# Decoder trunk on one core: memory heads and heads at other places of the second value stage, S1's output weights summed in SBUF, residual rows scaled on GpSimd

## The chip, the cores and the metric

The kernel runs on one core of a Trainium2 chip. The metric is the device time of one execution in microseconds (us), lower is better. The engines are called as the profile calls them: PE (TensorE, matrix products; PEld its weight loads), DVE (VectorE), ACT (ScalarE), POOL (GpSimd) and SP (SyncE, which here only issues DMAs). POOL also issues DMAs; only those can add to what lies at their target (accumulate).

## The reference

Two layers of a decoder over one sequence of 512 positions with 2048 columns, all in fp32:

```python
def hybrid_layer(h, mem, w_in, b_forget, w_mem_kv, w_out, ln_gain, ln_bias):
    p = h @ w_in                       # 2048 columns to all heads' parts and three small ones
    y_fox = forgetting_attention(q, k, v, cumsum(log_sigmoid(f_logit + b_forget)))   # 6 heads of 128
    y_dsa = sparse_attention(rope(q), rope(k), v, top_k of the index scores)         # 6 heads
    y_mem = attention(q, *split(mem @ w_mem_kv))                                     # 4 heads, 256 memory tokens
    y = concatenate([y_fox, y_dsa, y_mem]) * silu(gates)                             # 512 x 2048
    return layer_norm(ALPHA * h + y @ w_out, ln_gain, ln_bias)
```

A query of the sparse heads sees the 128 keys with the highest index score at most. Layer 2 takes layer 1's output.

## The kernel before

**Products.** PE multiplies a number as a high and a low part (`hi`, `lo`), so one fp32 product is three matmuls; ACT makes the high part of a weight (`whi<-raw`), DVE the low part (`wlo<-raw,whi`). In the trace these matmuls are triples such as z<-whi,yh, z<-wlo,yh, z<-whi,yl. The two large stages, the values (with gates and the projections that lie among them, PSUM tiles `v`) and the output projection (`z`), multiply 2 x 2 blocks with seven products instead of eight, whose names are P1, P7, Q6, Q4, P2, Q5, Q3. Some of them take a sum of weight blocks: `T1`, the right operand of Q5 (whose left operand is S1), is the sum of two blocks, as is `T3`, the operand of P7. Q6 and Q4 take a sum that grows from P7's (`grown`: an accumulating DMA of POOL adds a block to a tile in SBUF).

**Weights.** They stream in chunks of two halves; a half is 128 x 1024 (512 KB). `load_w` issues a chunk's load on SP (tiles `raw`) two chunks ahead of use, and the split runs three halves ahead. For the value stage's pairs 1 to 5, `pair_w` loads both blocks of a sum and DVE adds them (`raw<-raw,other`). For the value stage's pair 0 and all of the output stage, the sums are made in DRAM (`weight_sums`): POOL copies a block of 1 MB to a DRAM tile `sum` and later adds the other to it with an accumulating DMA; the halves are then loaded from `sum`. `paced` spreads these steps over the stages, and outside the first value stage each has a `pool_waits` ahead of it: DVE writes `mark`, POOL reads it into `seen`, so that POOL's queue goes no further than DVE has come.

**Stages of a layer.** Small and index products; the first value stage (`VAL_FIRST`, in all pairs P1, P7, P2, Q6, Q4); the second (`VAL_SECOND`, Q5 and Q3 of pairs 0 to 5, two chunks each, 24 in all, 24 matmuls each); the q and k projections of the heads that are not in the value products, with the attention heads run among them (the heads stage, tiles `c`, `s`, `pt`, `po`); the output stage (`OUT_ORDER`, steps of two chunks); the layer norm. In layer 2's first value stage `residual_rows` loads 12 tiles of layer 1's result, multiplies each by a row of gains and adds a row of biases (`scale_row`, on DVE) and writes it back with a POOL DMA.

**Heads.** A memory head (`mem_head`) loads its q by a turning DMA (DMA_TRANSPOSE on SP), splits it, multiplies by the memory keys (`sm`), turns the softmax's values on PE (`ptm`) and multiplies by the memory values (`po`). The others do the same with `s`, `pt` and `po`; `load_qk` and `load_ck` fetch their inputs on SP. `start_heads` queues the heads in the order of the table `START`. Memory heads 0 to 2 are queued at Q3 of pairs 1, 3 and 5, memory head 3 is the seventh in `START`.

**Order.** The program of each engine is written out once, at build time. `Clock` keeps an estimate of each engine's time; `flow` queues a generator of steps, and `advance`, called after each triple of matmuls or so, emits steps of queued work when their engine is due. So a head queued sooner moves its matmuls between other matmuls. On each engine, and on the two DMA queues, instructions go in program order. In the output stage `load_res` loads x's tiles (`z<-in_x_dram`, in layer 2 `z<-x`) on POOL, DVE adds them to the product (`z<-z,z`), and the splits of later weights stand behind that on DVE.

Of the kernel before, what the change touches and what calls it, by code (L numbers as in the profile page):

```python
# [16 lines left out]
ALU = mybir.AluOpType  # L17
# [22 lines left out]
R_ATTEND, R_QK, R_LOAD, R_MEM = 4, 5, 4, 8  # L40
# [14 lines left out]
         ("d", 4), ("d", 3), ("d", 5))  # L55
EARLY = 4
HEAD_CHUNKS = [(c + q, h) for c in ("f", "d") for h in range(EARLY, H_FOX) for q in ("q", "k")]
START = (("f", 0), ("f", 1), ("d", 0), ("f", 4), ("d", 1), ("f", 2), ("m", 3), ("f", 5), ("d", 2),
         ("f", 3), ("d", 4), ("d", 3), ("d", 5))
ACTIVE = 3  # L60
COUNTED = ("ck", "bt", "pr", "qh", "ql", "vraw", "tanh", "vh", "vl", "pthl", "y", "rope", "kmem", "vmem",
           "pm", "pth", "ptl", "yh", "yl")
# [29 lines left out]
PAIRS = 6  # L92
# [38 lines left out]
def stream():  # L131

    wall = all_chunks()
    where = {c: i for i, c in enumerate(wall)}
    out = []

    def product(kind, l, name, pair, gs=(0, 1)):
        right = PRODUCTS[name][2]
        for g in gs:
            at = lambda step: where[kind, l, 2 * pair + step[1], 2 * step[0] + g]  # L140
            if name in GROWN:
                of, step = GROWN[name]
                src = ("grown", (of, at(step)))
            elif kind == "val" and right in PAIRED and pair >= IN_DRAM:
                src = ("pair", tuple(at(step) for step in PAIRED[right]))
            elif isinstance(right, str):
                src = ("sum", (kind, l, right, pair, g))
            else:
                src = ("wall", at(right))
            out.append(({"val": "vs"}.get(kind, kind), l, (name, pair), g, src))  # L150

    for i, c in enumerate(wall):
        kind, l, j = c[:3]
        if kind == "out":
            if c == ("out", l, 0, 0):
                for name, pair in OUT_ORDER:
                    product("out", l, name, pair)
        elif kind == "val":
            if c == ("val", l, 0, 0):
                for order in (VAL_FIRST, VAL_SECOND):  # L160
                    for pair in range(PAIRS):
                        for name, g in order:
                            product("val", l, name, pair, (g,))
        else:
            out.append((*c, ("wall", i)))
    return out
# [81 lines left out]
def kernel(  # L248
# [32 lines left out]
    def slot(name, dt=F32, w=512):  # L281
        t = slots.tile([P, w], dt, tag="s", name=uid(name))
        if name in COUNTED:
            out_now.append(t)
        return t
# [5 lines left out]
    def enough(n):  # L291
        return now[1] == "out" or live() + n <= SLOTS - 2 * KT - 3
# [28 lines left out]
    chunks = stream()  # L321
# [16 lines left out]
    def half(src, h):  # L338
        return src[:, h * H:(h + 1) * H]

    def load_w(i, pieces=2, some=(0, 1)):
        if i < len(chunks) and chunks[i][4][0] != "grown":
            kind, key = chunks[i][4]
            src = {"wall": lambda: wall[key], "sum": lambda: sums[key],
                   "pair": lambda: wall[key[0]]}[kind]()
            if chunks[i][0] == "out" and chunks[i][2][0] == "P7":
                for h in some:
                    t = [slot("grown") for _ in range(2)]
                    raw.setdefault(i, []).append(t)
                    for c in range(2):  # L350
                        nc.sync.dma_start(t[c], half(src, h)[:, c * 512:(c + 1) * 512])
                return
            w = DM // pieces
            for c in range(pieces):
                if c * 2 // pieces not in some:
                    continue
                if c * 2 % pieces == 0:
                    raw.setdefault(i, []).append(raws.tile([P, H], F32, tag="raw", name=uid("raw")))
                nc.sync.dma_start(raw[i][-1][:, c * w % H:c * w % H + w], src[:, c * w:(c + 1) * w])
                if i < 3 and c * 2 % pieces == 0:  # L360
                    load_mem(2 * i + c * 2 // pieces)
                if kind == "pair":
                    for e in (2 * c, 2 * c + 1):
                        t = others[i, e] = slot("other")
                        nc.sync.dma_start(t, wall[key[1]][:, e * 512:(e + 1) * 512])

    others = {}


    def pair_w(n):  # L370
# [166 lines left out]
    def weight_sums(kind, l, names, pairs, some=(0, 1)):  # L537

        for name in names:
            for n in some:  # L540
                step = SUM_STEPS[name][n]
                for pair in pairs:
                    for g in range(2):
                        key = (kind, l, name, pair, g)
                        src = block(kind, l, pair, g, step)
                        if now[1] != "values":
                            pool_waits()
                        if n:
                            add_weights(key, src)
                        else:  # L550
                            sums[key] = dram.tile([P, DM], F32, name=uid("sum"))
                            nc.gpsimd.dma_start(sums[key], src)
                        yield

    def paced(gen, steps=PACE):

        n = 0
        for _ in gen:
            n += 1
            while now[1] in ("kv", "second", "heads"):  # L560
                yield 1
            yield {"out": 3, "index": 1 + n % 2}.get(now[1], steps)
# [7 lines left out]
    def all_sums():  # L570


        for l in range(DEPTH):
            yield from paced(value_sums(l))
            yield from paced(weight_sums("out", l, ("T3", "T1"), range(2)))
            while l + 1 < DEPTH and now[0] == l:
                yield 1

# [38 lines left out]
    def flow(gen, age=None, due=1e9):  # L617

        f = [0.0, gen, None, 0, None, clock.at["PE"] if age is None else age, due]
        flows.append(f)  # L620
        step_flow(f)
        return f
# [717 lines left out]
        yield "PE", 0, 0.0, lambda: len(started) >= n - 1 and enough(R_LOAD)  # L1340
        load_ck(l, h)

    def mem_turn(l, n, j):
        yield "PE", 0, 0.0, lambda: len(started) >= n and enough(R_MEM)
        started.append(("m", j))
        yield from mem_head(l, j)

    def start_heads(l):

        del started[:], working[:]  # L1350
        for n, key in enumerate(START):
            if key[0] == "m":
                flow(mem_turn(l, n, key[1]))
                continue
            if key[1] < EARLY:
                flow(fetched_head(l, n, key))
            elif key[0] == "f":
                flow(bias_only(l, n, key[1]))
            flow(attend(l, n, *key))
# [61 lines left out]
            yield 1  # L1421
        del rows["g", 3], rows["b", 3]

    def scale_row(t, c):
        nc.vector.tensor_tensor(t, t, rows["g", c], op=ALU.mult)
        nc.vector.tensor_tensor(t, t, rows["b", c], op=ALU.add)

    def residual_rows(l):

        tiles = [(st, c) for c in range(3) for st in range(4)]  # L1430
        t, scaled = {}, None
        for n in range(len(tiles) + 1):
            if n:
                st, c = tiles[n - 1]
                scaled = (st, c, t.pop(n - 1))
                scale_row(scaled[2], c)
                if st == 3:
                    del rows["g", c], rows["b", c]
            if n < len(tiles):
                st, c = tiles[n]  # L1440
                if st == 0:
                    load_row(l - 1, c, nc.sync)
                t[n] = slot("z")
                nc.sync.dma_start(t[n], x1_d[st * P:(st + 1) * P, c * 512:(c + 1) * 512])
            yield 1
            if scaled:
                st, c, d = scaled
                nc.gpsimd.dma_start(x1_d[st * P:(st + 1) * P, c * 512:(c + 1) * 512], d)
                scaled = d = None
            yield 2  # L1450
# [71 lines left out]
    for i, (kind, l, j, col, _) in enumerate(chunks):  # L1522
# [32 lines left out]
        for h in range(2):  # L1555
            n = 2 * i + h
            grow_w(n + 2)
            if i > 0:
                late_half = i > 8 and i + 2 < len(chunks) and chunks[i + 2][4][0] != "pair"
                if late_half:  # L1560
                    load_w(i + 2, 2, (h,))
                elif h == 0:
                    load_w(i + 2)
# [143 lines left out]
            begin(top_keys(l), whole=True)  # L1707
        if kind == "vs" and (name, pair, col) == ("Q6", 0, 1) and l > 0:
            begin(residual_rows(l), whole=True)
        if kind == "vs" and (name, pair, col) == ("Q5", PAIRS - 1, 1):  # L1710
            start_heads(l)
        if kind == "vs" and (name, col) == ("Q3", 1):
            if pair in (1, 3, 5):
                flow(mem_head(l, pair // 2))
        if kind == "vs" and (name, pair, col) == ("Q3", PAIRS - 1, 1):
            chains.clear()
            val_done.clear()
# [101 lines left out]
```

## Time and profile before

| | |
|---|---|
| time, median of 3 runs | 1930.95 us (1926.11 to 1932.08) |
| time of the profiled execution | 1930.1 us, span 1928.3 us |
| PE busy in the span | 1861.8 us, 97%, 8930 matmuls |
| DVE, ACT, POOL busy | 1598.3, 1086.7, 410.1 us |
| DMA | 480.49 MB, mean 249 GB/s |
| first value stage, layer 1 and 2 | 171 to 480 us, 1123 to 1446 us |
| second value stage | 482 to 622 us, 1446 to 1581 us |
| heads stage | 622 to 771 us, 1581 to 1730 us |
| output stage | 771 to 953 us, 1730 to 1917 us |

The span runs from the first to the last instruction of the profiled execution; the bounds of the stages are read off the trace by the tiles that PE writes. Nearly all instructions carry line 232, a helper that passes every call on, so groups are told apart by their tiles: `z<-wlo,yh` is a matmul into PSUM tile z from low weights and high y. In a stretch's row the share of an engine is its busy time over the length; the clock is the one that PE was granted, 1.00 at full speed.

### The profile page before, as it was taken

The page shows a single profiled execution, that of the slowest core. Times are in us where ns is not written, and L with a number is a line of the kernel's source. Part 1 is how long each engine was busy: PE and PEld are TensorE (multiplying, and loading weights), DVE is VectorE, ACT ScalarE, POOL GpSimd, SP SyncE. Part 2 cuts the span into 40 slices and gives each one's busy share as a digit, 9 for nine tenths or more (in the row PEclk, how much of TensorE's full clock was granted, in tenths as well). Part 3 has the DMA queues.
Part 4 walks back from the last instruction along what each step waited for, and adds up shares of the span by engine and source line. Part 5 has one row for each costly group of instructions (what it writes and reads, how often), then busy time and mean ns, then how long its engine had stood idle before and what let it go on. Part 6 is the DMA issues. An engine that isn't in the chain of part 4 may idle for free.

```text
span 1928.3 us, 26456 instructions
## 1 busy us (share of the span) xinstructions
PE 1861.8 (97%) x8930; PEld 1576.7 (82%) x8930; DVE 1598.3 (83%) x2575; ACT 1086.7 (56%) x1682; POOL 410.1 (21%) x571
## 2 busy tenths in 40 slices
PE   9999999999999999899999999999999999988897
PEld 8998888888887887777899987878888778877676
DVE  6789888999777888968887898889997778789598
ACT  5766455455555666644476754444455456576343
POOL 0111111112113122350021122122112132123511
PEclk9999999999999999999999999999999999999999
DMA  9885998879999664898597879999799995558986
GB/s 354 281 264 155 279 272 260 271 251 308 322 327 327 163 145 132 200 245 245 178 321 237 235 193 273 292 289 301 262 321 331 327 309 161 153 123 209 247 270 135
DMA packets 238693, 480.49 MB, mean 249 GB/s; under 512 B 94544, under 2 KB 110928, under 8 KB 234844
## 3 DMA queue, kind: packets, MB, share of 16 engines
q1 hardware_dynamic: 196476, 321.46, 51.8%
q0 software_dynamic: 41504, 156.29, 32.7%
q8 instruction: 70, 1.15, 0.2%
q10 hardware_dynamic: 576, 1.05, 0.1%
q14 instruction: 67, 0.55, 0.1%
HBM read 406.34 MB, written 105.93 MB: 266 GB/s over the span
## 4 chain that ended last, share of the span: by engine, by line
PE 66%; DMA 13%; DVE 12%; issue 5%; ACT 3%; SPq 1%; POOL 0%; DVEq 0%; ACTq 0%; POOLq 0%
PE v L232 30%; PE c L232 19%; PE z L232 8%; DMA other<-in_wall_dram 5%; DVE wlo L232 5%; DMA raw<-in_wall_dram 3%; DMA z<-x 3%; PE po L232 3%; PE s L232 2%; PE ix L232 2%; DVE raw L232 1%; DMA vraw<-vt 1%; DVE vraw L232 1%; ACT whi L232 1%; PE pt L232 1%
## 5 line engine op out<-in xcount | busy, mean ns | idle before, releaser
L232 ACT ACTIVATE whi<-raw 128x1024 fp32r<-128x1024 f32 (+1 forms) x497 | 523.3, 1056 | 439.3 <-PE v L232 215.9
L232 DVE TENSOR_TENSOR wlo<-raw,whi 128x1024 fp32r<-128x1024 f32 (+1 forms) x497 | 604.3, 1222 | 142.3 <-ACT whi L232 141.4
L232 PE MATMUL v<-wlo,vxh 128*128 128x512 f32 x768 | 299.3, 390 | 5.5 <-DVE wlo L232 5.5
L232 PE MATMUL v<-whi,vxh 128*128 128x512 f32 x768 | 300.3, 391 | 3.9 <-DVE vraw L232 3.9
L232 PE MATMUL v<-whi,vxl 128*128 128x512 f32 x768 | 299.0, 389 | 0.0
L232 PE MATMUL v<-wlo,xh 128*128 128x512 f32 x576 | 224.2, 389 | 0.1
L232 PE MATMUL v<-whi,xh 128*128 128x512 f32 x576 | 224.2, 389 | 0.0
L232 PE MATMUL v<-whi,xl 128*128 128x512 f32 x576 | 224.1, 389 | 0.0
L232 PE MATMUL c<-xh,whi 128*128 128x512 f32 (+1 forms) x544 | 200.4, 368 | 0.0
L232 PE MATMUL c<-xh,wlo 128*128 128x512 f32 (+1 forms) x544 | 198.2, 364 | 0.0
L232 PE MATMUL c<-xl,whi 128*128 128x512 f32 (+1 forms) x544 | 197.9, 364 | 0.0
L232 PE MATMUL z<-wlo,yh 128*128 128x512 f32 (+1 forms) x434 | 171.2, 395 | 19.9 <-DVE wlo L232 19.9
L232 PE MATMUL z<-whi,yl 128*128 128x512 f32 (+1 forms) x434 | 171.7, 396 | 13.7 <-DVE yl L232 13.7
L232 PEld LDWEIGHTS v<-wlo,vxh 128*128 128x128 f32 x768 | 144.2, 188 | 36.4 <-DVE wlo L232 7.2
L232 PEld LDWEIGHTS v<-whi,vxh 128*128 128x128 f32 x768 | 144.4, 188 | 36.1 <-issue 6.2
L232 PE MATMUL z<-whi,yh 128*128 128x512 f32 (+1 forms) x434 | 171.8, 396 | 0.7 <-ACT yh L232 0.7
L232 PEld LDWEIGHTS v<-whi,vxl 128*128 128x128 f32 x768 | 144.2, 188 | 30.0
L232 DVE TENSOR_TENSOR raw<-raw,other 128x512 f32<-128x512 f32 x160 | 105.1, 687 | 31.0 <-DMA other<-in_wall_dram 30.6
L232 PEld LDWEIGHTS v<-wlo,xh 128*128 128x128 f32 x576 | 108.1, 188 | 23.0 <-DVE wlo L232 0.5
L232 PEld LDWEIGHTS v<-whi,xh 128*128 128x128 f32 x576 | 108.1, 188 | 22.7
L232 PEld LDWEIGHTS v<-whi,xl 128*128 128x128 f32 x576 | 108.1, 188 | 22.4
L232 PEld LDWEIGHTS z<-wlo,yh 128*128 128x128 f32 x434 | 83.5, 192 | 38.2 <-DVE wlo L232 22.0
(198 smaller groups left out, 3420.5 us busy)
## 6 DMA issues: line engine op xcount, KB each, us to landing
raw<-in_wall_dram SPq DMA_DIRECT2D x371, 512.0 KB, 7.2
other<-in_wall_dram SPq DMA_DIRECT2D x160, 256.0 KB, 9.3
raw<-in_wall_dram POOLq DMA_DIRECT2D x56, 512.0 KB, 8.4
sum<-in_wall_dram POOLq DMA_DIRECT2D x24, 1024.0 KB, 12.1
v<-vraw POOLq DMA_DIRECT2D x72, 256.0 KB, 7.1
vt<-halves POOLq DMA_DIRECT2D x72, 256.0 KB, 6.7
raw<-sum SPq DMA_DIRECT2D x32, 512.0 KB, 8.5
grown<-in_wall_dram POOLq DMA_DIRECT2D x64, 256.0 KB, 11.9
```

The costliest lines, as they stand in the source:

```text
L232: return f(*args, **kw)
```

## The change

It has three parts. The number of matmuls is the same, 8713 rows of PE's program before and after.

**Heads.** The table `MEM_AT` queues the four memory heads at Q3 of pairs 0, 2, 3 and 4 (column 0 for pair 2, column 1 for the others); none is left in the heads stage, and the table `START` goes in favour of `HEADS`, the same order without the memory head. `HEADS_FROM` calls `start_heads` at Q3 of pair 4, column 1, two chunks ahead of Q5 of pair 5, column 1.

**T1 of the output stage.** Nothing is summed in DRAM for it. `load_both` loads the first block's half as two tiles of 128 x 512 (`both`) on SP, 12 halves ahead of use, and `add_both` adds the second block's with two accumulating DMAs on POOL, 8 halves ahead. Per layer this takes away four copies to `sum` and four adds on POOL with their `mark` and `seen`, and eight 512 KB loads of `sum`; it adds 16 SP loads and 16 POOL DMAs of 256 KB. ACT and DVE split these halves in two pieces of 512 columns.

**Residual rows.** The 24 operations of `residual_rows` run on POOL in place of DVE.

```diff
-START = (("f", 0), ("f", 1), ("d", 0), ("f", 4), ("d", 1), ("f", 2), ("m", 3), ("f", 5), ("d", 2),
-         ("f", 3), ("d", 4), ("d", 3), ("d", 5))
+BOTH_LOAD, BOTH_ADD = 12, 8
+HEADS_FROM = ("Q3", 4, 1)
+MEM_AT = {(0, 1): 0, (2, 0): 1, (3, 1): 2, (4, 1): 3}
...
+            elif kind == "out" and right == "T1":
+                src = ("both", tuple(at(step) for step in PAIRED[right]))
...
-        if i < len(chunks) and chunks[i][4][0] != "grown":
+        if i < len(chunks) and chunks[i][4][0] not in ("grown", "both"):
...
+    def load_both(n):
+
+        i, h = divmod(n, 2)
+        if i < len(chunks) and chunks[i][4][0] == "both":
+            t = raw.setdefault(i, [None, None])[h] = [slot("both") for _ in range(2)]
+            for c in range(2):
+                nc.sync.dma_start(t[c], half(wall[chunks[i][4][1][0]], h)[:, c * 512:(c + 1) * 512])
+
+    def add_both(n):
+
+        i, h = divmod(n, 2)
+        if i < len(chunks) and chunks[i][4][0] == "both":
+            src = half(wall[chunks[i][4][1][1]], h)
+            for c in range(2):
+                nc.gpsimd.dma_start(raw[i][h][c], src[:, c * 512:(c + 1) * 512], accum_op=ALU.add)
...
-            yield from paced(weight_sums("out", l, ("T3", "T1"), range(2)))
+            yield from paced(weight_sums("out", l, ("T3",), range(2)))
...
-    def mem_turn(l, n, j):
-        yield "PE", 0, 0.0, lambda: len(started) >= n and enough(R_MEM)
-        started.append(("m", j))
-        yield from mem_head(l, j)
...
-        for n, key in enumerate(START):
-            if key[0] == "m":
-                flow(mem_turn(l, n, key[1]))
-                continue
+        for n, key in enumerate(HEADS):
...
-    def scale_row(t, c):
-        nc.vector.tensor_tensor(t, t, rows["g", c], op=ALU.mult)
-        nc.vector.tensor_tensor(t, t, rows["b", c], op=ALU.add)
+    def scale_row(t, c, eng=nc.vector):
+        eng.tensor_tensor(t, t, rows["g", c], op=ALU.mult)
+        eng.tensor_tensor(t, t, rows["b", c], op=ALU.add)
...
-                scale_row(scaled[2], c)
+                scale_row(scaled[2], c, nc.gpsimd)
...
             grow_w(n + 2)
+            add_both(n + BOTH_ADD)
+            load_both(n + BOTH_LOAD)
...
-        if kind == "vs" and (name, pair, col) == ("Q5", PAIRS - 1, 1):
+        if kind == "vs" and (name, pair, col) == HEADS_FROM:
             start_heads(l)
-        if kind == "vs" and (name, col) == ("Q3", 1):
-            if pair in (1, 3, 5):
-                flow(mem_head(l, pair // 2))
+        if kind == "vs" and name == "Q3" and (pair, col) in MEM_AT:
+            flow(mem_head(l, MEM_AT[pair, col]))
```

**How it moves instructions.** PE at the end of layer 1's heads stage, before: a late head's last transposes (pt) and its first value products (po).

```order
L232 MATMUL pt_7485<-ident,bt_7169 128x128
L232 MATMUL pt_7485<-ident,bt_7171 128x128 x2
L232 MATMUL pt_7494<-ident,bt_7169 128x128
L232 MATMUL pt_7494<-ident,bt_7171 128x128
L232 MATMUL po_7512<-pthl_7490,vh_7473 128x512 x2
L232 MATMUL po_7512<-pthl_7490,vl_7474 128x512
L232 MATMUL po_7512<-pthl_7492,vh_7473 128x384 x2
```

The value products follow the transposes with nothing between them. PE at the first output products, after: the last transposes of a late head.

```order
L235 MATMUL pt_7670<-ident,pr_7514 128x128
L235 MATMUL pt_7670<-ident,pr_7505 128x128
L235 MATMUL z_7528<-whi_7436,yh_7560 128x512
L235 MATMUL z_7528<-wlo_7437,yh_7560 128x512
L235 MATMUL z_7528<-whi_7436,yl_7561 128x512
L235 MATMUL z_7527<-whi_7539,yh_7629 128x512
L235 MATMUL z_7527<-wlo_7540,yh_7629 128x512
L235 MATMUL z_7527<-whi_7539,yl_7630 128x512
```

Products of the output stage (z) follow the transposes, 21 rows of z and of the next head's scores (s) in all, and then come this head's value products. In the whole plan the last po of layer 1 stands behind 177 z matmuls before and 159 now.

POOL in layer 1's output stage, before: the last loads of x's tiles and what is queued around them.

```order
L232 TENSOR_TENSOR seen_8299<-mark_8298,mhalf 128x1
L232 DMA sum_4395<-in_wall_dram 128x2048
L232 DMA z_8307<-in_x_dram 128x512
L232 DMA z_8309<-in_x_dram 128x512
L232 DMA grown_7986<-in_wall_dram 128x512
L232 DMA grown_7987<-in_wall_dram 128x512
L232 DMA grown_8030<-in_wall_dram 128x512
L232 DMA grown_8031<-in_wall_dram 128x512
L232 TENSOR_TENSOR seen_8445<-mark_8444,mhalf 128x1
L232 DMA sum_4798<-in_wall_dram 128x2048
```

A 1 MB add to T1's sum stands ahead of the two loads of x, another behind the four grown adds. POOL at the same loads, after:

```order
L235 DMA z_8284<-in_x_dram 128x512
L235 DMA z_8286<-in_x_dram 128x512
L235 DMA grown_7985<-in_wall_dram 128x512
L235 DMA grown_7986<-in_wall_dram 128x512
L235 DMA grown_8025<-in_wall_dram 128x512
L235 DMA grown_8026<-in_wall_dram 128x512
L235 DMA both_8290<-in_wall_dram 128x512
L235 DMA both_8291<-in_wall_dram 128x512
```

The sums and their `seen` are gone, and the `both` adds stand behind the loads and the grown adds. On PE's scale these last two loads are issued some 53 matmuls ahead of the DVE additions that read them, 33 before; the first `both` adds are planned 91 matmuls ahead of ACT's first split.

POOL in layer 2's first value stage, after: the first residual tile.

```order
L235 TENSOR_TENSOR z_11252<-z_11252,row_11248 128x512
L235 TENSOR_TENSOR z_11252<-z_11252,row_11250 128x512
L235 DMA x_176<-z_11252 128x512
L235 DMA vt_167<-halves_11416 128x4x256
L235 DMA vt_167<-halves_11418 128x4x256
L235 DMA raw_11386<-in_wall_dram 128x1024
```

The two operations on z stood on DVE before, between the search for the top keys and the additions of weight pairs; now they stand on POOL ahead of the tile's write to x, of the writes of values (vt) and of a weight load. SP's loads for the first two heads and for memory head 3 (6 turning DMAs in all) move ahead of the last loads of weights of the second value stage.

## The prediction, made before the changed kernel was run

> **What bounds the kernel now.** I read the page's busy shares first, then the waits of TensorE (columns: total us, times, longest).
>
> ```profile
> span 1928.3 us, 26456 instructions
> PE 1861.8 (97%) x8930; PEld 1576.7 (82%) x8930; DVE 1598.3 (83%) x2575; ACT 1086.7 (56%) x1682; POOL 410.1 (21%) x571
> PE z L232 <- DVE wlo L232: 19.9, 4, 8.9
> PE z L232 <- DVE yl L232: 13.7, 7, 4.1
> PE v L232 <- DVE wlo L232: 5.5, 4, 1.6
> PE po L232 <- DVE pthl L232: 5.5, 4, 2.2
> PE ptm L232 <- DVE pm L232: 2.5, 3, 1.2
> ```
>
> TensorE is busy 97%. The change leaves its matmuls as they are, so a gain can only come out of the 66.5 us in which it idles, and out of the slower clock behind a long idle. More than half of that, 39.1 us, is three waits of the tail of the attention heads and of the output stage (z on wlo 19.9, z on yl 13.7, po on pthl 5.5). VectorE ends all three, so I ask what held VectorE. The stretches of each layer (first layer, then second; length, busy us and counts by engine, granted clock, DMA share, GB/s):
>
> ```profile
> 171.00:480.00 309.00, 309.00 (x1365) 255.84 (x1364) 274.28 (x399) 159.19 (x169) 60.25 (x82) 1.00 0.86 263
> 482.00:622.00 140.00, 136.95 (x614) 111.78 (x613) 100.55 (x133) 73.61 (x96) 30.00 (x40) 1.00 1.05 327
> 740.00:771.00 31.00, 27.94 (x149) 23.95 (x148) 22.65 (x58) 24.08 (x58) 5.64 (x7) 0.94 0.59 151
> 771.00:820.00 49.00, 42.42 (x199) 34.70 (x198) 44.34 (x77) 32.55 (x68) 18.78 (x24) 0.97 0.84 201
> 855.00:875.00 20.00, 11.08 (x42) 8.71 (x42) 7.20 (x13) 3.21 (x6) 4.03 (x5) 0.80 1.08 249
> 1123.00:1446.00 323.00, 317.12 (x1393) 260.66 (x1391) 295.33 (x433) 160.29 (x172) 66.89 (x94) 1.00 0.92 282
> 1446.00:1581.00 135.00, 131.34 (x588) 107.07 (x588) 94.79 (x125) 71.13 (x92) 28.60 (x39) 1.00 1.06 325
> 1700.00:1730.00 30.00, 26.72 (x143) 22.92 (x142) 22.57 (x57) 23.30 (x57) 5.54 (x7) 0.94 0.58 143
> 1730.00:1780.00 50.00, 43.21 (x207) 35.59 (x206) 44.84 (x77) 33.20 (x69) 19.30 (x23) 0.97 0.86 206
> 1811.00:1835.00 24.00, 14.50 (x58) 11.29 (x57) 12.38 (x21) 4.10 (x7) 9.22 (x12) 0.89 1.09 250
> ```
>
> The loss of a stretch is its length less TensorE's busy time, and that busy time times what the clock lacks to 1. Head tail, first layer: 31.00 − 27.94 = 3.1 and 0.06 × 27.94 = 1.7; 49.00 − 42.42 = 6.6 and 0.03 × 42.42 = 1.3: together 12.6. Second layer, in the same way: 3.3 + 1.6 + 6.8 + 1.3 = 13.0. The stretch of the output stage's residual: 8.9 + 0.20 × 11.08 = 11.1, and in the second layer 9.5 + 0.11 × 14.50 = 11.1. These two places hold 47.8 us; the first value stage of layer 1 holds nothing (309.00 of 309.00).
>
> In the tail the stalls are single matmuls behind VectorE, here of the first layer (start, duration, what, and in brackets the idle time before it):
>
> ```profile
> 757.60 0.58 PE L232 MATMUL po<-pthl,vh 128*128 128x512 f32 x1 [2.19 <-DVE pthl L232]
> 778.27 0.74 PE L232 MATMUL z<-whi,yl 128*128 128x512 f32 x1 [4.05 <-DVE yl L232]
> 871.85 0.80 PE L232 MATMUL z<-wlo,yh 128*128 128x512 f32 x1 [8.92 <-DVE wlo L232]
> ```
>
> The last heads' scores, transposes and values stand one behind the other with nothing between, while VectorE is busy 44.34 of 49.00 us. The third row is another case: wlo stands on VectorE behind a residual addition that waits for a load of x. The chain of work that ended last (start, duration), VectorE's row and GpSimd's queue there:
>
> ```profile
> 829.32 10.15 PE z L232 x45
> ...
> 856.99 13.42 DMA z<-in_x_dram
> ...
> 869.70 1.50 DVE L232 SCALAR_TENSOR_TENSOR z<-z,z 128x512 f32<-128x512 f32 x2 [12.54 <-DMA z<-in_x_dram]
> ...
> 850.84 1.52 POOL L232 TENSOR_TENSOR seen<-mark,mhalf 128x1 f32<-128x1 f32 x1
> 851.75 1.41 POOL L232 DMA_DIRECT2D sum<-in_wall_dram  x1
> 856.99 0.54 POOL L232 DMA_DIRECT2D z<-in_x_dram  x1 [2.03 <-DMA grown<-in_wall_dram]
> ```
>
> The z load is issued 5.2 us behind a 1 MB sum on the same queue and lands 13.42 us after its issue, with the DMA engines full (1.08).
>
> **The change, term by term.** The sum is made against the profiled execution, 1930.1 us, which is 0.85 under the median of the three.
>
> *Heads begun two chunks sooner, and memory head 3 moved to the second value stage.* TensorE now finds output matmuls between the transposes and the values of the last heads, and VectorE has one memory head less in the heads stage. Its whole price is the 25.6 us above; it can lose nothing there, since the work that it takes away is priced where it lands, in the third term (bounds −25.6 and 0). I take two thirds, −17: the plan's last value product still comes 159 z matmuls into the output stage, 177 before, so the tail is thinned and does not vanish, and VectorE's 44.34 of 49.00 stays near full. What is late next there is yl.
>
> *S1's output weights summed in SBUF.* Removed per layer: four 1 MB copies beside the value stage and four accumulating 1 MB adds with their mark and seen in the output stage, and eight 512 KB loads of the sums. Added: 16 loads of 256 KB on SP and 16 accumulating loads of 256 KB on GpSimd.
>
> ```profile
> grown<-in_wall_dram POOLq DMA_DIRECT2D x32, 256.0 KB, 12.1
> sum<-in_wall_dram POOLq DMA_DIRECT2D x4, 1024.0 KB, 9.8
> raw<-sum SPq DMA_DIRECT2D x8, 512.0 KB, 9.2
> ```
>
> (Those are the issues from 771 to 960 us: count, size, median us to landing.) The bytes of the output stage stay alike, 4 + 4 MB out and 4 + 4 MB in; only their order changes. The copies gone from the value stage give nothing, as TensorE is full there. In the output stage the adds no longer stand ahead of the last z loads, but behind them. In the order of the instructions these loads go out 53 matmuls ahead of their use, against 33: 20 × 10.15/45 = 4.5 us more. The sum at 851.75, 1 MB at 249 GB/s, is 4.2 us of DMA time that was ahead of them and is not now; I credit 1.5 of it, since SP's loads of `both` come into the same stretch. That is −6 a layer of 11.1, −12 in all. Bounds: −22.2 if the wait goes; +10 if `both` lands late in one layer, a stall like the 8.92 with its slow clock, and nothing else comes back. The adds go out 8 halves ahead, 91 matmuls or 20.5 us before the first split by ScalarE, against 12.1 to land for a grown add in that stretch; hence their cover. If that cover goes, Q5's split waits. Eight splits of 1024 columns per layer become sixteen of 512, as the grown ones are (1.29 for two at 841.70 against 1.227 for one, rows below): 8 × 0.06 = 0.5 us of VectorE per layer, hidden in the 79 us in which the output stage's rest runs without a stall.
>
> *The second value stage.* It takes one more memory head per layer, with its two transposes, and the first two heads' transposes two chunks sooner. TensorE and SP there:
>
> ```profile
> 1505.98 1.12 PE L232 MATMUL ptm<-ident,pm 128*128 128x128 f32 x4 [1.19 <-DVE pm L232]
> 558.84 4.97 SPq L1300 DMA_TRANSPOSE vraw<-vt  x1
> 598.60 6.06 SPq L1300 DMA_TRANSPOSE vraw<-vt  x2
> ```
>
> A memory head costs 1.19 us of wait here, and a transpose holds SP up to 5 us while raw loads stand behind it, in a stage with the DMA engines at 1.05 and 1.06. I take +2 a layer, +4. Bounds: −6.7 (the stage's whole idle time, 3.05 + 3.66, filled by the heads' work) and +14 (an uncovered transpose of 5 with two such waits in each layer).
>
> *Residual rows on GpSimd* (layer 2, first value stage, 24 instructions).
>
> ```profile
> L232 DVE TENSOR_TENSOR z<-z,row 128x512 f32<-128x512 f32 x40 | 27.3, 687 | 0.6
> L232 POOL TENSOR_TENSOR vl<-vraw,vh 128x512 fp32r<-128x512 f32 x24 | 35.3, 1469 | 159.6 <-ACT vh L232 159.6
> L232 DVE TENSOR_TENSOR wlo<-raw,whi 128x1024 fp32r<-128x1024 f32 x493 | 601.6, 1227 | 135.5 <-ACT whi L232 134.6
> 774.72 2.29 DVE L232 TENSOR_TENSOR wlo<-raw,whi 128x1024 fp32r<-128x1024 f32 x1
> 774.12 1.81 POOL L232 TENSOR_TENSOR vl<-vraw,vh 128x512 fp32r<-128x512 f32 x1 [8.43 <-ACT vh L232]
> 841.70 1.29 DVE L232 TENSOR_TENSOR wlo<-grown,whi 128x512 fp32r<-128x512 f32 x2 [0.83 <-ACT whi L232]
> 809.65 3.73 DVE L232 TENSOR_TENSOR wlo<-grown,whi 128x512 fp32r<-128x512 f32 x2
> 810.50 2.32 POOL L232 TENSOR_TENSOR vl<-vraw,vh 128x512 fp32r<-128x512 f32 x1
> ```
>
> VectorE loses 24 × 0.687 = 16.5 us. But a GpSimd tensor_tensor of this size stretches the VectorE operation that it meets: wlo at 774.72 took 2.29 against a mean of 1.227, and the pair at 809.65 took 3.73 against 1.29, 2.44 more. 24 × 1.06 = 25 us puts VectorE 9 us up, 24 × 2.44 = 59 puts it 42 up, in a stage with 323 − 295.33 = 27.7 us of slack. Few of the 24 meet the split that TensorE waits for: I take a third of 9, +3. Bounds: −5.9 (TensorE's idle time there, 323 − 317.12) and 42 − 27.7 = +14. GpSimd itself goes from 66.89 to about 102 of 323 us; behind its scaling stand writes of x and raw loads, covered by that slack.
>
> The Trainium skill, "SBUF — State Buffer", section "SBUF: two separate sides", has VectorE and GpSimd share one pair of ports under an exclusive lock, which a VectorE operation with two SBUF inputs needs too against a GpSimd operation that reads SBUF; the loser waits for the whole instruction. The two stretched rows agree. Taken strictly, each of the 24 blocks VectorE for up to 1.469 us, 35.3 less 16.5 = 18.8 us more VectorE, a third of which is +6, and the sum would be 3 us higher.
>
> Sum: −17 − 12 + 4 + 3 = −22; on the median, 1931 − 22 = 1909.
>
> **The rivals.**
>
> *The load wait only moves* (second term 0): the DMA engines stay full at 1.08 and 1.09, and the same megabytes must land; `both` or the grown adds are late instead of z. For it: the bytes are equal. Against: leads of 53 and 91 matmuls. 1909 + 12 = 1921, 20%.
>
> *The heads are not really sooner*: VectorE is the limit of the tail, and only 18 z matmuls (4 us) separate the two plans' last heads. The term is then −3 a layer: 1909 + 11 = 1920, 17%. Both together, 1932, no change, 8%.
>
> *All of both places goes*: −25.6 − 22.2 with nothing paid, 1883, 12%.
>
> *The other side: SP is held in the second value stage.* Six transposes (two of the memory head, four of the first two heads) come ahead of raw loads where the DMA engines have no room. At 4.97 us each, SP is held 30 us a layer. It decides once 17 of these 30 in each layer are not covered by loads already landed: 34 − 4 more than in my sum turns −22 into +8. In full it is 60 − 4 more, 1965; half way between the two, 1952. Against it: those four transposes are in this stage's last sixth already (598.60 of 482 to 622), and raw loads are issued two chunks of 24 matmuls ahead of use, 10.8 us, more than one transpose holds. 6%.
>
> **How the numbers follow.** My forecast has what is left, 37%, its own range 1898 to 1917 (the head tail from −25 to −10, the others by a few us). The range 1886 to 1925 leaves out half of the all-gone case (6%), both failures together (8%) and the SP case (6%). 0.3%, which a measurement of this kernel can tell, is 5.8 us: faster means under 1925. The forecast, the two single failures and the all-gone case hold 86%, of which 3 lie in their upper edges: 83% faster, 10% the same (8 and 2), 7% slower (6 and 1).
>
> **What would show it.** Right: po on pthl and z on yl fall from 19.2 us to about 7; the z wait on wlo falls from 19.9 to about 9, and VectorE's 12.54 behind the z load is halved; the second stage's waits of ptm rise to about 5; wlo in the second layer's value stage has a higher mean. Wrong: a wait of z on `both`'s wlo of 9 us or so; a tail from 740 to 820 that still lacks 9 us; v waiting on raw loads by more than 10 us a layer; v on wlo rising by over 10 us.

## The result and the profile after

The changed kernel takes 1942.5 us (median of 5 runs, 1939.98 to 1945.3) against 1930.95 before: 1.0065 times the time before, 95% interval 1.0047 to 1.0084. I had forecast 1909, in a range of 1886 to 1925. It is 12 us slower.

The page of the profiled execution after, and TensorE's waits. In the later kernels the helper that passes every call on is line 235 or 236; SPq is SP's queue.

```profile
span 1940.7 us, 26586 instructions
PE 1864.1 (96%) x8930; PEld 1577.0 (81%) x8930; DVE 1604.3 (83%) x2557; ACT 1089.3 (56%) x1698; POOL 449.9 (23%) x601
PE v L235 <- DVE vraw L235: 29.4, 6, 14.0
PE pt L235 <- ACT bt L235: 12.2, 2, 8.1
PE z L235 <- DVE wlo L235: 10.0, 15, 2.2
PE z L235 <- ACT whi L235: 4.5, 6, 1.1
PE sm L235 <- DVE ql L235: 4.1, 2, 2.3
PE z L235 <- DVE yl L235: 1.5, 2, 0.7
```

The waits that the forecast wanted gone are gone: z on yl fell from 13.7 to 1.5, po on pthl from 5.5 to nothing shown, z on wlo from 19.9 with a longest of 8.9 to 10.0 with a longest of 2.2. In their place stand two that were small or absent: v on vraw (a sum in PSUM tile v that cannot start before VectorE has emptied the one ahead of it), 3.9 before and 29.4 now, and pt on bt, 12.2. Both lie at the seam of the second value stage and the heads stage. The stretches after (columns as in the prediction):

```profile
600.00:660.00 60.00, 39.98 (x170) 32.80 (x169) 29.77 (x57) 29.55 (x57) 15.40 (x28) 0.80 0.67 187
740.00:790.00 50.00, 50.00 (x259) 42.93 (x258) 49.39 (x91) 31.85 (x68) 6.42 (x7) 1.00 0.59 141
786.00:835.00 49.00, 47.43 (x237) 39.58 (x236) 46.71 (x86) 37.65 (x82) 21.49 (x25) 1.00 0.91 225
835.00:860.00 25.00, 25.00 (x115) 20.89 (x115) 20.26 (x35) 13.22 (x24) 14.59 (x19) 1.00 1.08 243
890.00:920.00 30.00, 23.93 (x90) 15.98 (x89) 19.50 (x33) 12.44 (x20) 3.27 (x4) 1.00 0.86 230
1123.00:1446.00 323.00, 322.06 (x1420) 265.58 (x1419) 304.94 (x417) 165.73 (x180) 106.17 (x118) 1.00 0.90 272
1560.00:1630.00 70.00, 46.77 (x215) 38.41 (x214) 38.67 (x69) 35.71 (x69) 20.01 (x32) 0.83 0.70 176
1748.00:1800.00 52.00, 50.73 (x256) 42.48 (x255) 49.72 (x96) 39.82 (x84) 21.49 (x26) 1.00 0.90 221
```

The tail of the heads (740 to 835, 1748 to 1800) now lacks 1.6 and 1.3 us of TensorE, where it lacked 12.6 and 13.0. The z load's stretch (835 to 860) is full. But from 600 to 660 TensorE is idle for 20.0 us and, by the prediction's sum, loses 0.20 × 39.98 = 8.0 more by its clock; in the second layer it is 23.2 and 8.0. That sum makes the clock's part too large: from the first layer's second value stage to z 193 (the way of the table below) TensorE's busy time is 344.18 us before and 345.45 after, so 10.6 of the 11.9 us by which it is longer are idle time.

To compare kernels whose orders differ I took from each trace the start of four matmuls that stand behind the same work in each: the first of the second value stage's 576, the 193rd and the 385th into z of the output stage, and the last into z. us between them, first and second layer:

| kernel | second stage to z 193 | z 193 to 385 | z 385 to the last | to layer 2's second stage |
|---|---|---|---|---|
| before | 357.1, 357.6 | 55.3, 55.6 | 65.1, 69.1 | 481.7 |
| changed | 369.0, 367.6 | 43.5, 47.6 | 74.9, 75.0 | 476.6 |
| heads' part alone | 370.5, 367.6 | 52.3, 54.3 | 65.1, 66.8 | 481.1 |
| T1's part alone | 356.5, 359.0 | 43.5, 47.4 | 75.8, 78.0 | 476.4 |
| rows' part alone | 355.8, 358.0 | 55.1, 55.6 | 65.1, 69.0 | 481.1 |
| late start | 352.1, 353.2 | 43.5, 45.0 | 76.8, 76.9 | 478.8 |
| late start, loads early | 354.5, 352.8 | 43.5, 46.6 | 76.1, 76.7 | 476.4 |
| late start, loads in place | 354.8, 354.8 | 43.5, 45.4 | 76.3, 77.2 | 478.6 |
| no scores early | 361.4, 363.1 | 43.5, 47.2 | 77.8, 75.6 | 478.8 |
| later start, both sooner | 355.6, 352.5 | 43.5, 46.8 | 72.3, 74.0 | 478.8 |

Changed against before: 11.9 + 10.0 lost from the second stage to z 193, 11.8 + 8.0 won at the z loads, 9.8 + 5.9 lost again behind them, 5.1 won on the way to the second layer's second stage: +12.4 with the rest, the difference of the spans.

Where the loss starts, in the trace of the changed kernel: TensorE's stalls, SP's queue, and VectorE's and ScalarE's order at the first of them (start, duration, what; in brackets the idle time before).

```profile
622.72 0.76 PE L235 MATMUL v<-whi,vxh 128*128 128x512 f32 x1 [14.02 <-DVE vraw L235]
657.06 2.05 PE L235 MATMUL pt<-ident,bt 128*128 128x128 f32 x8 [4.17 <-ACT bt L235]
1583.93 0.76 PE L235 MATMUL v<-whi,vxh 128*128 128x512 f32 x1 [12.86 <-DVE vraw L235]
1620.05 2.05 PE L235 MATMUL pt<-ident,bt 128*128 128x128 f32 x8 [8.07 <-ACT bt L235]
...
599.21 5.26 SPq L1319 DMA_TRANSPOSE vraw<-vt  x2
605.19 4.17 SPq L1319 DMA_TRANSPOSE vraw<-vt  x2
610.03 1.37 SPq L362 DMA_DIRECT2D raw<-in_wall_dram  x3
625.22 0.80 SPq L1272 DMA_DIRECT2D vraw<-v  x2
...
616.12 1.06 ACT L235 ACTIVATE whi<-raw 128x1024 fp32r<-128x1024 f32 x1 [9.86 <-DMA raw<-in_wall_dram]
...
617.21 1.23 DVE L235 TENSOR_TENSOR wlo<-raw,whi 128x1024 fp32r<-128x1024 f32 x1 [9.57 <-ACT whi L235]
618.95 1.22 DVE L235 TENSOR_TENSOR wlo<-raw,whi 128x1024 fp32r<-128x1024 f32 x1
620.68 1.29 DVE L235 TENSOR_TENSOR ql<-vraw,qh 128x512 fp32r<-128x512 f32 x2
621.88 1.28 DVE L235 TENSOR_TENSOR vraw<-vraw,v 128x512 f32<-128x512 f32 x2
```

SP is held by the four transposes of the first two heads (with two loads of ck, an input of their bias) until 609.4 and only then issues three raw loads. ScalarE waits 9.86 us for the first. VectorE has to empty the accumulator v (vraw<-vraw,v adds it to the base, the part of this sum that an earlier stage left in DRAM and that SP loads as vraw<-v) before TensorE may open the next sum there, but that stands on VectorE behind both splits of those raw loads, behind the memory head's own steps and behind the early heads' ql (the low part of a q or k). So TensorE stands 14.02 us. Then SP's next loads of the base wait until 625.22, and raw loads behind them with it.

### The profile page after: what moved, and what is told of

Its sections match the earlier page's. It is cut to its first block, busy times and chain, and to the rows that moved or that the text cites. A ratio compares the mean times of both kernels' runs of the same rounds, so it can differ in the third digit from the quotient of the medians.

```text
span 1940.7 us, 26586 instructions
## 1 busy us (share of the span) xinstructions
PE 1864.1 (96%) x8930; PEld 1577.0 (81%) x8930; DVE 1604.3 (83%) x2557; ACT 1089.3 (56%) x1698; POOL 449.9 (23%) x601
## 5 line engine op out<-in xcount | busy, mean ns | idle before, releaser
L235 ACT ACTIVATE whi<-raw 128x1024 fp32r<-128x1024 f32 (+1 forms) x481 | 506.6, 1057 | 456.9 <-PE v L235 211.0
L235 PE MATMUL v<-whi,vxh 128*128 128x512 f32 x768 | 302.2, 393 | 29.4 <-DVE vraw L235 29.4
L235 POOL DMA_DIRECT2D v<-vraw x72 | 47.5, 682 | 314.8 <-DVE vraw L235 190.8
```

The source lines that it names most:

```text
L235: return f(*args, **kw)
```

## The experiments

Each kernel was timed in 5 rounds beside the kernel before, on one chip for each group; between groups, times are compared as ratios to before (0.001 is 1.9 us). Theory A, formed from the trace above, was that the turning DMAs hold SP ahead of the raw loads, and that this is the whole loss.

**The parts alone, and the late start.** The first three are the kernel before with one part of the diff. The fourth changes one line of the changed kernel:

```diff
-HEADS_FROM = ("Q3", 4, 1)
+HEADS_FROM = ("Q5", 5, 1)
```

> Before, with the heads' part of the change alone (MEM_AT, HEADS_FROM), T1 and residual rows as before. Theory A (the six turning DMAs hold SP ahead of the last raw loads of the second value stage): the stage costs about 24 us more per layer, the tail gives 13 back, so about 1931 + 2 x 11 = 1953 us, v waiting on a raw load by 13 to 14 us once per layer. Rival B (the stall needs the other parts too, through the full DMA engines): no such wait, 1905 to 1915 us.

Measured: 1943.24 against 1928.61, ratio 1.008 (1.0068 to 1.0093). It is 15 us slower, 10 less than expected; the waits are those of the changed kernel (v on vraw 28.6, pt on bt 11.4), without the other parts. The heads' part makes the loss.

> Before, with T1 summed in SBUF alone. If the trace of the changed kernel reads right, the z load's wait goes (-12 and -8 us) and waits for the both adds come (+10 and +6): 1931 - 4 = about 1927 us. If the sums made the room for the transposes, about 1905 to 1910.

Measured: 1926.95, ratio 0.9987 (0.9977 to 0.9997). That is 2.5 us less by the ratio, where the reading of the trace had 4: small, as it said, and far from the other branch.

> Before, with the residual rows on GpSimd alone. If the 5.1 us that the second layer's first value stage is shorter by come from this part: 1926 us, PE's waits of v on wlo near 1 us. If from the copies to sum that are gone: 1931 us or, by the stretched VectorE operations, up to 1934.

Measured: 1926.71, ratio 0.9989 (0.9977 to 1.0): no measurable change. The time is that of the first branch, but its sign is missing: v waits 4.4 us on wlo, not near 1. The table gives the 5 us of the first value stage to T1's part (476.4) and not to this one (481.1); in the other traces with T1's part this way took 476.4 to 480.6, so the 5 us are the upper end of what that part gives. The splits over the whole kernel, and the stage as a stretch:

```profile
L232 DVE TENSOR_TENSOR wlo<-raw,whi 128x1024 fp32r<-128x1024 f32 x493 | 617.9, 1260 | 134.3 <-ACT whi L232 133.1
```

```profile
1123.00:1446.00 323.00, 318.38 (x1395) 260.69 (x1394) 299.50 (x408) 161.74 (x172) 107.60 (x119) 1.00 0.92 288
```

The mean split rose from 1227 to 1260 ns, 16.3 us over all 493. (In the traces of T1's part alone and the heads' part alone it is 1226 and 1224, in the changed kernel and the late start 1257 and 1265.) VectorE, freed of 16.5 us, is 4.2 us busier in that stage (299.50 against 295.33), and TensorE is not held up by it.

> The changed kernel with the heads begun at Q5 of pair 5, column 1, as before; the four memory heads stay in the second value stage. Theory A with the first two heads' four transposes as the cause: the 13 to 14 us wait of v goes, the tail keeps half of its gain (no memory head in it): 1905 to 1915 us. Rival C (memory head 3's transposes and loads in the second stage are the cause): the wait stays, 1935 to 1945 us.

Measured: 1915.9, ratio 0.9938 (0.9923 to 0.9953). The start two chunks earlier is what makes the changed kernel slow: 1.0065 against 0.9938 is 24 us. Rival C falls: the memory heads are all in the second stage here.

**Is it the transposes?** A table issues `load_qk` of the first two heads by itself, and these heads then skip their own. The next run does so with the heads begun late; the two behind it put the loads at Q3 of pairs 3 and 4, column 0, one with the heads begun late, one with them begun as in the change:

```diff
+FETCH_AT = {("Q3", 4, 1): (0, 1)}
...
+        if kind == "vs" and (name, pair, col) in FETCH_AT:
+            for k in FETCH_AT[name, pair, col]:
+                load_qk(HEADS[k])
```

> The late start (Q5 of pair 5, column 1), but the four turning DMAs of the first two heads stand on SP where the change put them, at Q3 of pair 4, column 1, with no head begun there. Theory A (these transfers hold SP ahead of raw loads, whatever the heads do): v waits 12 to 14 us once per layer again, 1916 + 2 x 10 = about 1936 us. Rival D (the early heads' own scores, softmax and bias work delay the splits on ScalarE and VectorE): no wait, 1912 to 1918 us.

Measured: 1915.96, ratio 0.9939 (0.9923 to 0.9954). Theory A in its simple form falls. And yet the wait came:

```profile
615.10 0.77 PE L236 MATMUL v<-whi,vxh 128*128 128x512 f32 x1 [9.20 <-DVE vraw L236]
...
594.97 5.74 SPq L1320 DMA_TRANSPOSE vraw<-vt  x4
601.86 2.15 SPq L363 DMA_DIRECT2D raw<-in_wall_dram  x4
```

In the late start the same matmul waited 2.17 us. So the hold of SP goes with a wait of 9 us, but this one is given back: where the late start has its own waits later (ptm on pm 2.33 at 627.33, po on pthl 7.6 in all), this kernel has none.

> As the run with early loads, but two of the four turning DMAs at Q3 of pair 3, column 0, and two at Q3 of pair 4, column 0: the same four transfers in the same stage, no more than three in a row. Theory A in its form 'four to six in a row outlast the raw loads that are ahead': 1912 to 1918 us. Form 'each one costs its hold of 3 to 5 us in a full stage': as the early loads, about 1936 us.

Measured: 1919.89, ratio 0.9948 (0.9936 to 0.996), against 0.9939 and 0.9938 the same within the intervals.

> The changed kernel (heads begun at Q3 of pair 4, column 1), with the first two heads' four turning DMAs spread over pairs 3 and 4 in the same way. Theory A: the 13 to 14 us waits go, the tail keeps its gain: 1942 - 2 x 14 = 1914, less if the wait of pt on bt (4 and 8 us) came from the same hold: 1905 to 1914 us. Rival D: about 1942 us.

Measured: 1946.65, ratio 1.0091 (1.0076 to 1.0107). Spreading the transposes does not repair the early start. The wait of v halved to 6.72 at the same place, but ptm waited 4.06 and pt on bt 13.0 us in all. Together with the early loads this speaks for rival D: it is what the early heads do, not their loads alone.

> The late start with T1 summed in DRAM as before: the price of the T1 part beside the other two. By the traces (z load -12 and -8 us, both adds +10 and +6) the part is worth 2 us per layer: 1916 + 4 = 1920 us. If the both adds only took the wait over: 1916.

Measured: 1928.72, ratio 1.0 (0.9987 to 1.0012). Both branches missed: beside the late start, T1's part is worth 12 us, alone 2.5.

**Which of the early heads' work?** With no scores early, `ready` of an attention head also asks that the stage is heads or out, so that loads and splits stay early. The second run is T1 and rows without the heads' part. The other two change the constants named.

```diff
-            return (len(started) >= turn_no and len(working) < ACTIVE
+            return (now[1] in ("heads", "out") and len(started) >= turn_no and len(working) < ACTIVE
```

> The changed kernel (start at Q3 of pair 4, column 1), but the heads' scores and all that follows them wait for the heads stage; their loads and the splits of q and k stay early. Theory E (the early heads' scores, softmax and turns stand in PE's, ACT's and DVE's order ahead of the last chunks' work and wait there): about 1916 us, like the early loads alone, and no wait of pt on bt. Theory F (the splits of q and k on ScalarE and VectorE, ahead of the emptying of v, do it): v still waits 12 us or more per layer, 1935 to 1943 us.

Measured: 1934.44, ratio 1.0031 (1.0018 to 1.0044). Between the two: no wait of pt on bt, but v waits 27.8 us. On VectorE and SP (the emptying of v stands behind ql, and SP's second loads of the base go out at 621.61):

```profile
617.08 1.28 DVE L235 TENSOR_TENSOR ql<-vraw,qh 128x512 fp32r<-128x512 f32 x2
618.28 1.27 DVE L235 TENSOR_TENSOR vraw<-vraw,v 128x512 f32<-128x512 f32 x2
...
607.55 1.37 SPq L362 DMA_DIRECT2D raw<-in_wall_dram  x3
621.61 0.80 SPq L1272 DMA_DIRECT2D vraw<-v  x2
622.46 2.29 SPq L362 DMA_DIRECT2D raw<-in_wall_dram  x4
```

> T1 and residual rows of the change, heads wholly as before. Against the late start (1916) it tells what the four memory heads in the second value stage are worth. If the parts add: 1929 - 2 - 2 = 1925 us, and the memory heads' move is worth 9 us. If the T1 part alone made the late start faster: 1916.

Measured: 1924.65, ratio 0.9992 (0.9981 to 1.0003). The memory heads' move is worth 10 us beside T1's part, and nothing without it (the late start without T1, 1.0).

> The changed kernel with the heads begun at Q3 of pair 5, column 0, three chunks later than the change and one later than before. If a start that leaves the second stage free is what helps: 1912 to 1917 us, waits of v below 4 us. If the tail needs the earlier start: 1920 us or more, with po on pthl back.

Measured: 1912.94, ratio 0.9921 (0.9907 to 0.9934). The wait of po on pthl is back (8.5 us) and v on vraw is 9.9 in all, both against the first branch; yet the time is within it, and the least of this group.

> The late start with the both tiles loaded 16 and added 12 halves ahead instead of 12 and 8. If the adds were late for want of lead: the waits of z on both's splits (about 10 us per layer) fall to under 4, 1905 to 1910 us. If the DMA engines are full there: the wait returns at the z loads, 1914 to 1920 us.

Measured: 1914.43, ratio 0.993 (0.9916 to 0.9943), the same as the late start. From z 385 to the last the time fell (76.8 to 72.3, 76.9 to 69.3), from z 193 to 385 it rose (43.5 to 45.2, 45.0 to 52.8): the wait moved to the loads ahead. The median landing of the both adds went from 17.0 to 12.7 us.

**The place in the queue, and the way to a faster kernel.** Loads in place: as the early loads, but each `load_qk` in a queued step, so that it stands where the change has it.

```diff
+    def fetch_early(key):
+        yield "PE", 0, 0.0
+        load_qk(key)
...
-                load_qk(HEADS[k])
+                flow(fetch_early(HEADS[k]))
```

> The late start, with the first two heads' four turning DMAs on SP exactly where the change has them (behind one raw load, ahead of three raw loads and of the next two loads of the base, vraw<-v), without their loads of ck and with no split or score begun early. The early loads stood four places further ahead and cost nothing in all. If the place in SP's queue makes the loss of the run without scores (1934): 1930 to 1936 us. If the splits of q and k ahead of the emptying of v make it: 1914 to 1920 us.

Measured: 1919.42, ratio 0.9964 (0.9951 to 0.9978): 5 us of the 18 of the run without scores (an interval that just touches the late start's), the other 13 are not SP's place. The same stall is 9.44 us, and the second loads of the base go out at once:

```profile
615.93 0.77 PE L236 MATMUL v<-whi,vxh 128*128 128x512 f32 x1 [9.44 <-DVE vraw L236]
...
597.01 8.10 SPq L1320 DMA_TRANSPOSE vraw<-vt  x4
605.17 1.52 SPq L363 DMA_DIRECT2D raw<-in_wall_dram  x3
606.86 1.18 SPq L1273 DMA_DIRECT2D vraw<-v  x2
```

> The changed kernel with the heads begun one chunk later (Q5 of pair 5, column 0), one chunk before the old place: two more raw loads go ahead of the four turning DMAs. If the loss grows evenly with the chunks of an earlier start (26 us for two): about 1929 us. If it comes only once the raw loads and the base of the last pair stand behind them: 1914 to 1920 us.

Measured: 1915.65, ratio 0.9941 (0.9929 to 0.9954), the late start's height: the loss sets in with the second chunk.

> The best parts together: heads begun at Q3 of pair 5, column 0, both tiles loaded 14 and added 10 halves ahead. If the two gains add (1913 and 1914 against 1916): 1909 to 1913 us, ratio to before about 0.991. If they meet in the full DMA engines: 1914 to 1918 us.

Measured: 1910.67, ratio 0.9918 (0.9905 to 0.9931). It beats both kernels: 17 us under before, and by the ratios 0.9918/1.0065 = 0.985 of the changed one. From the later start alone (0.9921) it cannot be told apart, so a gain from the sooner adds is not shown. Its waits are small ones:

```profile
PE po L235 <- DVE pthl L235: 8.5, 2, 4.3
PE v L235 <- DVE vraw L235: 8.2, 6, 3.3
PE z L235 <- DVE wlo L235: 6.6, 10, 1.6
```

## Why the prediction was wrong

*Third term, +4: the step that failed.* The second value stage cost not 2 but about 22 us a layer: the 11.9 and 10.0 of the table, with the 11.0 and 11.7 that the tail gave back on the same way by the prediction's sums (19 a layer, if the tail is counted by idle time alone). I priced one wait for the memory head and less than one transpose. The row of 4.97 us behind that price was itself a wait, in SP's queue from 555 to 566 us before:

```profile
SPq L1300 <- PE v L232: 5.0, 1, 5.0
```

What the runs show in place of the +2, in ratios to before: late start 0.9938; the first two heads' loads early but ahead of everything, 0.9939; in their place in the queue, 0.9964 (+5 us); their loads of ck and their splits early too, 1.0031 (+13); their scores and softmax too, 1.0065 (+6.6). The rival with SP had the place and the sign right (v waiting at the end of this stage; it was to decide from 17 us a layer), and had 6%; its mechanism is the smaller part. The hold of SP starts the stall, 9 us of it. The rest goes with a loop through SP's queue that is in no term of mine; SP's waits from 600 to 630 us after:

```profile
SPq L1272 <- PE po L235: 13.7, 1, 13.7
...
SPq L1319 <- PE v L235: 2.3, 1, 2.3
SPq L1319 <- DVE vraw L235: 1.5, 2, 1.1
```

The last two rows say that 3.8 us of the hold itself were waits and not transfers. The first row is the loop: the next loads of the base wait 13.7 us for a value product of the memory head (po), which stands on TensorE behind the stalled v, and the raw loads stand behind them. At this place such a wait for the memory head, of 11 us or more in one piece, is there in each layer of all four kernels with the start of the change (heads' part alone, changed, spread, no scores), and in no other run is any over 7. With the loads in place but nothing else early it is gone, and with it the 13 us; but that run has no early splits and no early loads of ck either. So the shares of this wait and of the splits ahead of the emptying of v are not separated, and stay open. With the scores early too, pt waits for a softmax that has been put off.

*First term, −17.* The mechanism was right: the tail's 25.6 us fell to 2.9, −22.7 by the prediction's sums. Of idle time alone it is 19.7 to 2.8, −16.9, so whether the size was too small hangs on the clock's part.

*Second term, −12.* The z load's wait went (11.8 and 8.0 between z 193 and 385; in the second layer not all of it), and the both adds took most of it back (9.8 and 5.9). The measured sum is −4. The step that failed is the cover of the adds. I set 12.1 us to landing, from the grown adds, against a lead of 20.5 us; the issues of the changed kernel say 17.0, and the first add had a lead of 14.8:

```profile
both<-in_wall_dram SPq DMA_DIRECT2D x32, 256.0 KB, 9.9
both<-in_wall_dram POOLq DMA_DIRECT2D x32, 256.0 KB, 17.0
...
866.37 0.86 POOL L235 DMA_DIRECT2D both<-in_wall_dram  x1 [1.10 <-DMA grown<-in_wall_dram]
...
881.15 0.63 ACT L235 ACTIVATE whi<-both 128x512 fp32r<-128x512 f32 x1 [1.41 <-DMA both<-in_wall_dram]
```

Nor was it one late add, as my bound of +10 had it: the 16 adds of that layer landed one by one from 881.04 to 915.20 us, 2.3 us apart, and each split of them waited for its own landing.

So the rival with the wait that only moves was mostly right, at 20%. What I costed at nothing, the copies gone from the value stage, is the likely source of the 5 us that the changed kernel won ahead of the second layer's second stage (1 to 5 in the traces with T1's part); no run tried the copies alone.

*Fourth term, +3.* No loss that can be measured: the interval of the rows' part alone ends at 1.0. The operations took longer on GpSimd than the row that I used (1469 ns):

```profile
L235 POOL TENSOR_TENSOR z<-z,row 128x512 f32<-128x512 f32 x24 | 41.5, 1730 | 2.3 <-DMA z<-x 1.2
```

The stretch of VectorE came, at half the size (+4.2 us of busy time against my 9); its price to TensorE did not. With the rows' part alone the stretch is 16.5 + 4.2 = 20.7 us, 0.86 for each of the 24. The Trainium skill ("SBUF — State Buffer", "SBUF: two separate sides") lets the loser of the shared ports wait for the whole instruction, which would be up to 1.73 here; the runs agree with a wait, and show about half of that on average. No run shows why it is only half.

The sum of what was measured: −22.7 + 44.6 − 4 − 5.1 = +12.8, against 12.4 of the spans. It is the sum of the table over again, since the 44.6 has the 22.7 in it, and proves no single term. The range failed because the third term's bound, +14, was drawn from single rows of SP, one transpose at a time; the heads' work and the loads of the base queued behind four of them have no row in the profile of before.

Open: why the memory heads' move pays 10 us with T1's part and nothing without. In the traces the two late starts differ by 5 to 6 us from the second stage to z 193, and in the first layer TensorE's waits account for only some 2 of them (z on yl 1.9).

## What to carry to other kernels

A chain of work begun sooner fills a gap at its end only if every engine and queue that it passes has room at its new start: ask, for each in-order queue, what of the critical work stands behind the new entries, above all who empties the accumulator that the next matmul needs, and whether an entry in turn waits for the engine that it is to feed. A stall that a transfer makes may be given back later, so a wait in the trace is no proof of its price; move that one transfer alone and time it. And where one change has a part that gains and a part that loses, try its starting point at each step in between: one chunk less took the loss away.

## What was not expected of the hardware

A GpSimd tensor_tensor of 128 x 512 took 1730 ns in this stage (z<-z,row) against 1469 for those of before (vl<-vraw,vh), and with 24 of them VectorE's 493 splits took 16.3 us longer in all, as much as was taken off VectorE. The accumulating loads of 256 KB went out some 2 us apart when they were back to back, and took a median of 17.0 us to land where the grown adds of the output stages before took 12.1. And a row of SP that reads as a transfer of 4.97 us was, by SP's waits (5.0), all but wholly a wait.
